# Accumulating transfers for two of four weight sums and wide products in an FFN's first chunk, with a rearranged start and tail

## The chip, the cores and the metric

One core of a Trainium2 chip runs the kernel. Its engines are named as in the profile: PE (TensorE matmuls; PEld their weight loads), DVE (VectorE), ACT (ScalarE), POOL (GpSimd) and SP (SyncE, which issues most DMAs). The metric is the device time of one execution in microseconds; the median of 3 runs before the change is 2033.53 us.

## The reference

One layer of a hybrid encoder, batch 1, 512 tokens, width 2048, all in float32:

```
xn    = rms_norm(x, g1);  proj = xn @ w_in            (2048 -> 5120)
y_a   = silu(layer_norm(depthwise_conv31(u * sigmoid(gate))))   1024 channels
y_b   = neighbourhood_attention(q, k, v, rpb)                   16 heads of 64
x     = x + concat(rms_norm(y_a), rms_norm(y_b)) @ w_out
h     = rms_norm(x, g2) @ w_up                        (2048 -> 2 x 5632)
h     = depthwise_conv3(h);  h = silu(h_gate) * h_value
x     = x + h @ w_down                                (5632 -> 2048)
out   = rms_norm(x, g3)
```

## The kernel before

**Exact products.** A float32 operand is split into a high part `hi` that PE's fast format (fp32r) holds and a low part `lo`, the rest. A product is then three matmuls, hi·hi, hi·lo and lo·hi (`mm3`, L127, L128, L129). Weights arrive as tiles of 128x1024 (512 KB) by DMAs that SP issues; `parts` (L113 to L118) makes `hi` by an ACT copy (L116) and `lo` by a DVE subtraction (L117). Four buffers hold the split pairs, seven hold raw tiles and the sums `ws` that are made of them. A written-out list `plan` holds the weights of all products in the order of their use; `weights()` issues a load and its split three products ahead (AHEAD = 3). Small steps of other stages (statistics, norms) are generators; `tick` lets one step through behind a named matmul, and each `yield` in a generator leaves its rest to a later tick. `pin` fixes an instruction's place on its engine; the others are placed by a scheduler.

**Start (L214 to L255).** x arrives as 16 tiles of 128x512 (k = 0 to 15), each split by ACT (L249) and DVE (L250) with the gain g1, which a DMA of ACT's queue brings. The weights of the first two projections arrive in ten pieces, two of each size, between the tiles of x, and are split at L226 and L227. Idle matmuls (L236, L240) run on PE until the first pieces are there.

**group_a (L373 to L402)** makes the convolution branch's layer norm and RMS norm. Their sums over channels are made by PE (`rsqrt_steps`, L190), the root by DVE and ACT (L173 to L177), and a broadcast by PE (L207). Two yields stand ahead of the layer norm's root, and two (RA_AFTER) ahead of the RMS norm's.

**FFN.** 44 blocks f of 128 hidden channels, gate and value each, come in 11 chunks of four. The up-projection of an f is done by a scheme with seven products in place of eight: K is halved, the tokens are halved, and products c = 0 to 6 use the weights A22, s = A21 + A22 (L666), A21 + A11 (L668), A11, s + A11 (L673), A12 and s + A12 (L677). The sums are DVE additions of 128x1024. Two forms exist:

- `up_apart` (L793 to L832, used for f0 to f3): a product is 24 matmuls of 256 columns. Its bank is emptied by ACT copies (L823, L826) or DVE additions (L825 to L831). For f0 the first three products run side by side, since their inputs are still being made.
- `up` (L708 to L791, f4 on): the high and low parts of the input stand side by side in 512 columns, so that a product is 8 wide matmuls of 512 columns (L718) and 8 of 256 for the low weights (L724). Its result has two halves, which ACT copies (L750) and more DVE additions (L765 to L789) put together.

`hidden` (L844) multiplies with the norm's factor, applies the convolution over tokens (L838 to L840), the gate's Silu (L849) and the product (L850); `in_two` splits it into `hh` and `hl` (L855, L856). From f4 on, products of the down-projection of the chunk before stand between the up products (`behind`, `down`, L859 to L871): ACT copies a bank out and POOL issues a 256 KB DMA that adds it to the residual in DRAM (L871). The first of them follows the third product of f4.

**stats2 (L644 to L653)** makes the RMS norm ahead of the FFN; its steps run beside f0's products, and f0's results wait for its broadcast (L207, L211).

**Tail (L941 to L998).** The last down products of the first 384 tokens are added, and their norm's statistics made (`rsqrt_steps`, rstd3). Meanwhile the last 128 tokens are computed the other way round, as four banks `pt` of 128 tokens x 512 channels (L973 to L979). A step of `spread` behind each block of three matmuls makes the statistics and finishes the transposed output (`finish`: L935 on DVE, L932 and L933 on ACT and POOL; DMAs L937 and L939). The 128 tokens' squares are summed on ACT (L981), the root is made (L986 to L989, L173 to L177) and four tiles are scaled and written (L993 to L998).

Of the kernel before, what the change touches and what calls it, by code (L numbers as in the profile page):

```python
# [16 lines left out]
P = 128  # L17
# [37 lines left out]
RA_AFTER = 2  # L55

PCOLS = [("g1", KD), ("dww", NC_ * CK), ("dwb", NC_), ("lng", NC_), ("lnb", NC_), ("cog", NC_),
# [10 lines left out]
def layer(ctx: ExitStack, tc: tile.TileContext, xT, xG, w_in, w_v, w_out, w_up, w_down, par, tab, g3, out, last_out):  # L68
# [27 lines left out]
    pin(nc.scalar.dma_start(g1, par[:, POFF["g1"]:POFF["g1"] + KD]))  # L96
# [5 lines left out]

    ones_r = consts.tile([P, P], F32R, name="ones")
# [112 lines left out]
    early = [[], []]  # L216

    def piece(u, j, c0, c1):

        if c0 == 0:  # L220
            early[j].append((t4([P, U * P], "raw"), wpool.tile([P, U * P], F32R, tag="whi", name="whi", bufs=NW),
                             wpool.tile([P, U * P], F32R, tag="wlo", name="wlo", bufs=NW)))
        n = (NC_, 0)[j]
        raw, hi, lo = (t[:, c0 * P:c1 * P] for t in early[j][u])
        pin(nc.sync.dma_start(raw, w_in[n, :, (u * U + c0) * P:(u * U + c1) * P]))
        pin(nc.scalar.activation(hi, raw, AF.Copy))  # L226
        pin(nc.vector.tensor_sub(lo, raw, hi.bitcast(F32)))  # L227
# [4 lines left out]
    warm = t2("warm", F32R)  # L232
    pin(nc.vector.tensor_copy(warm.rearrange("p (i k) -> p i k", k=P), ones.unsqueeze(1).broadcast_to([P, S // P, P])))
    ps = psa.tile([P, 2, S], F32, tag="sc", name="idle")
    for n in (S, S) + 3 * (H,) + 3 * (H - 32,):
        pin(nc.tensor.matmul(ps[:, 0, :n], warm[:, :P], warm[:, :n], start=True, stop=True))  # L236
    for n in (S, S) + 4 * (H,):
        for j in range(2):
            rows = slice(j * DH, (j + 1) * DH)
            pin(nc.tensor.matmul(ps[:, j, :n], warm[rows, :P], warm[rows, :n], start=True, stop=True))  # L240


    pieces = {k: [(u, j, c0, c1) for j in range(2)]
              for k, u, c0, c1 in ((0, 0, 0, 2), (2, 0, 2, 4), (4, 0, 4, 8), (6, 1, 0, 4), (9, 1, 4, 8))}
    for k in range(KD):
        x1.append(t2("x"))
        last = pin(nc.sync.dma_start(x1[k], xG[k]))
        h, l = t2("xh", F32R), t2("xl", F32R)
        pin(nc.scalar.activation(h, x1[k], AF.Copy, scale=g1[:, k:k + 1]))  # L249
        pin(nc.vector.scalar_tensor_tensor(l, x1[k], g1[:, k:k + 1], h.bitcast(F32), op0=ALU.mult, op1=ALU.subtract))  # L250
        xs.append((h, l))
        for c in pieces.get(k, ()):
            piece(*c)
# [73 lines left out]
    def project_first():  # L327
# [4 lines left out]
        for kk in range(KD):  # L332
            for j in range(2):
                m = mm3(both[j], early[j][kk // U][1:], kk % U, xs[kk][0], xs[kk][1], kk == 0, kk == KD - 1)
            if kk % 4 == 3:
                tick(m)
# [35 lines left out]
    def group_a():  # L372
# [15 lines left out]
        yield  # L388
        yield
# [9 lines left out]
        for _ in range(RA_AFTER):  # L399
            yield  # L400
# [243 lines left out]
    def stats2():  # L644
# [8 lines left out]
        rstd2.append((yield from rsqrt_steps(acc2, D, "rstd2", free=True, rest=2)))  # L653

    def factors(f):
# [4 lines left out]

        def make(c):
            if c == 0:
                return load(A22)
            if c == 1:
# [128 lines left out]
    def up_apart(f, between):  # L793

        def begin(c):
            return weights(), (psa.tile([P, S], F32, tag="po", name="pu") if c == 6 else
# [47 lines left out]
    def hidden(f, between):  # L844
        g, v = (up_apart if f < CH else up)(f, between)
# [33 lines left out]

    for c in range(NCH):  # L880
        hs = []
        for i in range(CH):

            last = c == NCH - 1 and i == CH - 1
            if c and i == CH - 1:
                hs = [in_two(h) for h in hs]
            hs.append(hidden(c * CH + i, lambda at: None if last else behind(c, i, at)))
# [185 lines left out]
```

## Time and profile before

| what | value |
|---|---|
| median of 3 runs | 2033.53 us (2030.55 to 2034.37) |
| profiled execution | 2030.16 us |
| its span | 2028.4 us |
| granted TensorE clock, mean | 0.998 |
| ACT busy | 1050.9 us (52%) |
| POOL busy | 159.5 us (8%) |
| HBM | 220.04 MB read, 54.53 MB written |

The span is the time from the first to the last record of the profiled execution; the rest of its time lies around it. A row of the timeline has the start and the duration in us, the engine, the line and the operation, output <- input with sizes, the count of instructions that follow one another, and in brackets the idle time before it and what ended that. A row of a group has the count, the busy time in us, the mean in ns, and the idle time before it. A row of the waits has total us, times, and the longest. A matmul's duration includes its way through the array, so the pace of PE is read from the starts: 0.227 us for 512 columns and 0.12 us for 256.

### The profile page before, as it was taken

Reading aid. Unit: us, or ns where it says so; the run is one execution under the profiler, and the core shown is the slowest. Engines: PE = TensorE matmul, PEld = TensorE weight load, DVE = VectorE, ACT = ScalarE, POOL = GpSimd, SP = SyncE. Lnnn points to the kernel's source line nnn. Section 1 sums busy time; section 2 is a strip of 40 time slices with the busy share of each in tenths; the row PEclk is TensorE's granted clock in tenths of the full one; section 3 lists DMA queues with packets and bytes.
Section 4 is the critical chain, followed back from the end, with each engine's and each line's share of the span. In section 5 each row is a group of like instructions: output and inputs, shape, how many; then the busy total and the mean of one; then the engine's idle time right before and its main releaser. Section 6 shows DMA issues by size and latency. Waiting matters only on the chain.

```text
span 2028.4 us, 28313 instructions
## 1 busy us (share of the span) xinstructions
PE 2015.4 (99%) x10672; PEld 1726.5 (85%) x10672; DVE 1675.5 (83%) x2298; ACT 1050.9 (52%) x1674; POOL 159.5 (8%) x188
## 2 busy tenths in 40 slices
PE   9999999999999999999999999999999999999998
PEld 7888888888888998888888888888888888888887
DVE  7986888988577898888888888888888888889875
ACT  7323344466346555555555555555555555555563
POOL 0000000000001001111111111111111111110111
PEclk9999999999999999999999999999999999999999
DMA  7232333336347435566565565565565565564583
GB/s 256 83 104 84 114 94 109 109 124 215 108 120 178 120 114 146 123 147 146 125 146 146 128 142 146 128 142 146 121 149 146 125 146 146 127 144 127 144 206 126
DMA packets 97784, 276.41 MB, mean 136 GB/s; under 512 B 10992, under 2 KB 12784, under 8 KB 97648
## 3 DMA queue, kind: packets, MB, share of 16 engines
q1 hardware_dynamic: 72288, 228.45, 36.3%
q0 software_dynamic: 25216, 46.15, 15.5%
q8 instruction: 84, 1.38, 0.3%
q14 instruction: 52, 0.43, 0.1%
q10 hardware_dynamic: 144, 0.01, 0.0%
HBM read 220.04 MB, written 54.53 MB: 135 GB/s over the span
## 4 chain that ended last, share of the span: by engine, by line
PE 96%; DVE 2%; DMA 1%; ACT 0%; issue 0%; SPq 0%; ACTq 0%; DVEq 0%
PE pu L718 25%; PE pu L724 13%; PE pd L129 8%; PE pd L127 8%; PE pd L128 8%; PE pj L127 5%; PE pj L128 5%; PE pj L129 5%; PE po L127 3%; PE po L128 2%; PE po L129 2%; PE pv L313 1%; PE pv L312 1%; PE pv L314 1%; PE pu L127 1%; PE pu L129 1%
## 5 line engine op out<-in xcount | busy, mean ns | idle before, releaser
L116 ACT ACTIVATE whi<-raw 128x1024 fp32r<-128x1024 f32 x364 | 384.4, 1058 | 503.8 <-PE pj L128 136.6
L117 DVE TENSOR_TENSOR wlo<-raw,whi 128x1024 fp32r<-128x1024 f32 x364 | 444.4, 1221 | 214.0 <-ACT whi L116 205.2
L718 PE MATMUL pu<-xc,whi 128*128 128x512 f32 x2240 | 552.9, 391 | 0.0
L718 PEld LDWEIGHTS pu<-xc,whi 128*128 128x128 f32 x2240 | 413.0, 188 | 79.1
L724 PEld LDWEIGHTS pu<-xc,wlo 128*128 128x128 f32 x2240 | 292.3, 191 | 13.9
L724 PE MATMUL pu<-xc,wlo 128*128 128x256 f32 x2240 | 296.6, 283 | 0.0
L129 PE MATMUL pd<-hh,wlo 128*128 128x512 f32 x640 | 250.1, 391 | 0.0
L127 PE MATMUL pd<-hh,whi 128*128 128x512 f32 x640 | 249.6, 390 | 0.0
L128 PE MATMUL pd<-hl,whi 128*128 128x512 f32 x640 | 249.3, 390 | 0.0
L871 POOL DMA_DIRECT2D x2d<-pdc x160 | 139.4, 873 | 1162.4 <-ACT pdc L870 837.4
L128 PE MATMUL pj<-xl,whi 128*128 128x512 f32 x512 | 200.2, 391 | 0.1
L129 PE MATMUL pj<-xh,wlo 128*128 128x512 f32 x512 | 200.0, 391 | 0.0
L127 PE MATMUL pj<-xh,whi 128*128 128x512 f32 x512 | 198.9, 393 | 0.0
L750 ACT ACTIVATE pl<-pu 128x256 f32<-128x256 f32 x280 | 104.6, 382 | 143.5 <-PE pu L718 136.4
L116 ACT ACTIVATE whi<-ws 128x1024 fp32r<-128x1024 f32 x132 | 139.8, 1059 | 75.2 <-PE pu L718 58.2
L366 DVE SCALAR_TENSOR_TENSOR y<-ch,prm,y 128x500 f32<-128x500 f32 (+14 forms) x240 | 173.3, 740 | 4.3
L117 DVE TENSOR_TENSOR wlo<-ws,whi 128x1024 fp32r<-128x1024 f32 x132 | 161.1, 1220 | 13.9 <-ACT whi L116 13.6
L129 PEld LDWEIGHTS pd<-hh,wlo 128*128 128x128 f32 x640 | 120.1, 188 | 28.5 <-DVE wlo L117 3.3
L128 PEld LDWEIGHTS pd<-hl,whi 128*128 128x128 f32 x640 | 120.2, 188 | 24.9 <-DVE hl L856 0.3
L127 PEld LDWEIGHTS pd<-hh,whi 128*128 128x128 f32 x640 | 120.4, 188 | 22.6
L870 ACT ACTIVATE pdc<-pd 128x512 f32<-128x512 f32 x160 | 93.8, 588 | 79.3 <-PE pd L129 65.9
L127 PEld LDWEIGHTS pj<-xh,whi 128*128 128x128 f32 x512 | 96.3, 188 | 20.7 <-ACT xh L249 0.2
(204 smaller groups left out, 2886.4 us busy)
## 6 DMA issues: line engine op xcount, KB each, us to landing
raw<-in_w_up SPq DMA_DIRECT2D x176, 512.0 KB, 3.7
raw<-in_w_down SPq DMA_DIRECT2D x88, 512.0 KB, 4.0
x2d<-pdc POOLq DMA_DIRECT2D x160, 256.0 KB, 4.8
raw<-in_w_in SPq DMA_DIRECT2D x60, 512.0 KB, 3.8
raw<-in_w_out SPq DMA_DIRECT2D x32, 512.0 KB, 3.8
raw<-in_w_v SPq DMA_DIRECT2D x16, 512.0 KB, 4.1
tab<-in_tab SPq DMA_DIRECT2D x32, 256.0 KB, 5.0
x<-in_xG SPq DMA_DIRECT2D x16, 256.0 KB, 5.4
```

Source lines behind the costliest of these rows:

```text
L116: i = nc.scalar.activation(hi[:, :n], raw[:, :n], AF.Copy)
L117: j = nc.vector.tensor_sub(lo[:, :n], raw[:, :n], hi[:, :n].bitcast(F32))
L127: nc.tensor.matmul(ps, hi[:, a], mh, start=start, stop=False)
L128: nc.tensor.matmul(ps, hi[:, a], ml, start=False, stop=False)
L129: return nc.tensor.matmul(ps, lo[:, a], mh, start=False, stop=stop)
L312: nc.tensor.matmul(ps, xh, wh[:, f], start=kk == 0, stop=False)
L366: nc.vector.scalar_tensor_tensor(y[:, a:b], h[:, a + j - PAD:b + j - PAD], prm[:, o + j:o + j + 1], y[:, a:b], op0=ALU.mult, op1=ALU.add)
L718: i = nc.tensor.matmul(ps, w[0][:, k * P:(k + 1) * P], comb[c][k], start=k == 0, stop=stop and k == ks[-1])
L724: i = nc.tensor.matmul(ps[:, H:], w[1][:, k * P:(k + 1) * P], comb[c][k][:, :H], start=False, stop=stop and k == U - 1)
L750: nc.scalar.activation(to, ps, AF.Copy)
L870: nc.scalar.activation(t, ps, AF.Copy)
L871: nc.gpsimd.dma_start(xd[d], t, accum_op=ALU.add)
```

## The change

Six parts:

1. **Start.** g1 is joined to the first tile of x (128x528, one DMA); ACT's DMA goes. The first split's high part is made by DVE. The weights of the first two projections lie interleaved in a new array `w_a` and come in five DMAs for k = 0, 1 to 3, 4 to 7, 8 to 11 and 12 to 15, issued behind x0, x1, x2, x6 and x10. The idle matmuls are six of 512 and one of 256 columns.
2. **group_a.** Three yields ahead of the layer norm's root in place of two; one ahead of the RMS norm's in place of two.
3. **stats2 and f0.** stats2's broadcast is four ticks behind its root in place of two. f0's gating and convolution are issued behind the second product of f1. f0's product c = 3 uses a bank of the pool "po" (before, c = 6 did).
4. **Wide products** (`up`) for f1 to f3.
5. **Sums by transfers** for f0 to f3: A22 is loaded a second time, into `ws`, and POOL issues two accumulating DMAs of 512 KB, A21 onto `ws` and A11 onto A21's tile. The DVE additions L666 and L668 go for these f.
6. **Tail.** The four banks alternate between two pools; the statistics' last part and all of `finish` come from the third bank's third step on, two calls a step; the sum of the first three squares stands ahead of the third bank's gain; the last root is written out, with a factor of -0.5 beside the square root.

```diff
+    xg0 = t4([P, U * P], "raw")[:, :S + KD]
+    pin(nc.sync.dma_start(xg0, x0))
...
-    pieces = {k: [(u, j, c0, c1) for j in range(2)]
-              for k, u, c0, c1 in ((0, 0, 0, 2), (2, 0, 2, 4), (4, 0, 4, 8), (6, 1, 0, 4), (9, 1, 4, 8))}
+    pieces = {0: (0, 1), 1: (1, 4), 2: (4, 8), 6: (8, 12), 10: (12, 16)}
...
-        yield
-        yield
+        for _ in range(3):
+            yield
         r = yield from rsqrt_steps(acc, CONV, "rln")
...
-        for _ in range(RA_AFTER):
-            yield
+        yield
         ra.append((yield from rsqrt_steps(acc, CONV, "ra")))
...
-        rstd2.append((yield from rsqrt_steps(acc2, D, "rstd2", free=True, rest=2)))
+        rstd2.append((yield from rsqrt_steps(acc2, D, "rstd2", free=True, rest=4)))
...
+        def sums():
+            a["s"] = t4([P, U * P], "ws")
+            nc.sync.dma_start(a["s"], w_up[f, A22])
+            nc.gpsimd.dma_start(a["s"], w_up[f, A21], accum_op=ALU.add)
+            load(A21)
+            nc.gpsimd.dma_start(a[A21], w_up[f, A11], accum_op=ALU.add)
+
         def make(c):
             if c == 0:
-                return load(A22)
-            if c == 1:
+                load(A22)
+                if f < CH:
+                    sums()
+                return a[A22]
+            if c == 1 and f < CH:
+                load(A11)
+            elif c == 2 and f < CH:
+                return a[A21]
+            elif c == 1:
                 a["s"] = t4([P, U * P], "ws")
                 add(a["s"], load(A21), a[A22])
...
-            return weights(), (psa.tile([P, S], F32, tag="po", name="pu") if c == 6 else
+            return weights(), (psa.tile([P, S], F32, tag="po", name="pu") if c == (6 if f else 3) else
...
     def hidden(f, between):
-        g, v = (up_apart if f < CH else up)(f, between)
+        return gated_tile(f, *up(f, between))
+
+    def gated_tile(f, g, v):
...
+    def meanwhile(c, i, at):
+        if (c, i, at) == (0, 1, 1):
+            hs[0] = gated_tile(0, *hs[0])
+        behind(c, i, at)
...
+            if not c and not i:
+                hs.append(up_apart(0, lambda at: None))
+                continue
...
-        elif (g, k) == (1, 0):
+        elif (g, k) == (2, 2):
...
-        elif rb and pairs:
-            at = pairs.pop(0)
+        for at in pairs[:2 if rb else 0]:
+            pairs.remove(at)
             finish(at, rb[at % 3 == 1], at % 3 == 1, at % 3 != 1)
...
-    root(r, y, v)
+    nc.scalar.activation(r, v, AF.Sqrt)
+    nc.vector.tensor_scalar(v, v, -0.5, None, op0=ALU.mult)
+    nc.vector.reciprocal(r, r)
+    nc.vector.scalar_tensor_tensor(y, r, v, r, op0=ALU.mult, op1=ALU.mult)
+    nc.vector.scalar_tensor_tensor(y, y, 1.5, r, op0=ALU.add, op1=ALU.mult)
```

More of the change, by code (lines that the diff above doesn't have):

```diff
@@ L215, in layer @@
     acc1 = t2("acc1")
[L216 to L227, printed above, removed]
+    early = []
@@ new lines, in layer, with piece @@
+    xg0 = t4([P, U * P], "raw")[:, :S + KD]
+    pin(nc.sync.dma_start(xg0, x0))
+    def piece(k0, k1):
+        if k0 % CH == 0:
+            early.append((t4([P, U * P], "raw"), wpool.tile([P, U * P], F32R, tag="whi", name="whi", bufs=NW),
+                          wpool.tile([P, U * P], F32R, tag="wlo", name="wlo", bufs=NW)))
+        o = k0 // CH * U * P
+        pin(nc.sync.dma_start(early[-1][0][:, 2 * k0 * P - o:2 * k1 * P - o], w_a[:, 2 * k0 * P:2 * k1 * P]))
+        for k in range(k0, k1):
+            if k % 2 and k > k0:
+                continue
+            raw, hi, lo = (t[:, 2 * k * P - o:2 * min(k // 2 * 2 + 2, k1) * P - o] for t in early[-1])
+            pin(nc.scalar.activation(hi, raw, AF.Copy))
+            pin(nc.vector.tensor_sub(lo, raw, hi.bitcast(F32)))
@@ L251, in layer @@
         xs.append((h, l))
-        for c in pieces.get(k, ()):
-            piece(*c)
+        if k in pieces:
+            piece(*pieces[k])
+        if k == 0:
+            pin(nc.vector.tensor_copy(g1, xg0[:, S:]))
     with tc.issue_after(last.ins):
```

60 lines of the change are left out of this document (33 added, 27 removed).

## The prediction

> **What bounds the kernel now.** First the profiled page: its busy line, the chain that ended last, and the loads of weights.
>
> ```profile
> PE 2015.4 (99%) x10672; PEld 1726.5 (85%) x10672; DVE 1675.5 (83%) x2298; ACT 1050.9 (52%) x1674; POOL 159.5 (8%) x188
> ...
> PE 96%; DVE 2%; DMA 1%; ACT 0%; issue 0%; SPq 0%; ACTq 0%; DVEq 0%
> ...
> raw<-in_w_up SPq DMA_DIRECT2D x176, 512.0 KB, 3.7
> ```
>
> TensorE (PE) is busy 99% of 2028.4 us and is 96% of the chain. So a change pays only where PE stands still, or where its own matmuls become fewer or shorter. An average of 83% on VectorE (DVE) hides stages, so I next cut the FFN's first chunk into windows: the third to seventh product of f0, f1 to f3, and the wide f4 up to its first down products.
>
> ```profile
> core 0: us, PE busy (x) PEld busy (x) DVE busy (x) ACT busy (x) POOL busy (x), PEclk, DMA share, GB/s
> ...
> 680.60:692.80 12.20, 12.19 (x102) 12.19 (x103) 9.95 (x17) 4.88 (x7) 0.00 (x0) 1.00 0.30 86
> 692.80:754.30 61.50, 61.45 (x510) 61.19 (x510) 60.87 (x79) 32.47 (x41) 0.00 (x0) 1.00 0.36 112
> 754.30:766.30 12.00, 12.00 (x66) 10.19 (x65) 11.83 (x17) 9.62 (x16) 0.00 (x0) 1.00 0.29 89
> ```
>
> Here both engines are full: DVE works 60.87 of 61.50 us beside f1 to f3. Over the 85.7 us it is busy 9.95 + 60.87 + 11.83 = 82.65 and idle 3.05. The waits of 676 to 768 us and the chain in it show where PE and DVE meet:
>
> ```profile
> PE pu L127 <- ACT vv L823: 1.5, 1, 1.5
> PEld pd L128 <- DVE hl L856: 0.3, 1, 0.3
> ...
> 680.61 0.39 PE pu L127
> 681.11 0.12 PE pu L129
> ...
> 754.48 2.07 PE pu L718 x9
> 756.55 1.91 PE pu L724 x16
> ```
>
> PE loses one block of 1.5 us ahead of 680.61: f0's fourth product waits for a bank that ACT empties. And at the first down products it already waits 0.3 us for a `hl` of DVE: the two engines arrive there together.
>
> **The change, part by part.** All terms are against the profiled execution, 2030.16 us (span 2028.4 and 1.8 around it); the median of the three runs is 2033.53, to which I apply the sum at the end.
>
> (a) *PE's own work in chunk 0.* f0's fourth product goes to another, free bank: -1.5 to -1.7. The wide form replaces 24 matmuls of 256 columns by 8 of 512 and 8 of 256: 8 x 2.07/9 + 8 x 1.91/16 = 2.80 us a product, against 24 x 0.12 = 2.88. The window 692.80 to 754.30 holds 21 apart products with two broadcasts of 0.23, (61.5 - 0.5)/21 = 2.90. So 21 x 0.10 = -2.1 at most, -1.7 at least. Alone PE would gain 3.2 to 4.2 us.
>
> (b) *DVE's work there.* The groups of 692.8 to 754.3, and two starts on DVE:
>
> ```profile
> L666 DVE TENSOR_TENSOR ws<-raw 128x1024 f32<-128x1024 f32 x3 | 3.7, 1218 | 0.0
> L668 DVE TENSOR_TENSOR raw<-raw 128x1024 f32<-128x1024 f32 x3 | 3.7, 1217 | 0.0
> L825 DVE TENSOR_TENSOR vl<-vv,pu 128x512 f32<-128x512 f32 x3 | 2.0, 681 | 0.0
> L827 DVE TENSOR_TENSOR uu<-uu,pu 128x256 f32<-128x256 f32 x3 | 1.2, 414 | 0.0
> ...
> 685.19 1.23 DVE L117 TENSOR_TENSOR wlo<-ws,whi 128x1024 fp32r<-128x1024 f32 x1 [1.13 <-ACT whi L116]
> ...
> 691.47 1.23 DVE L117 TENSOR_TENSOR wlo<-raw,whi 128x1024 fp32r<-128x1024 f32 x1 [1.13 <-ACT whi L116]
> ```
>
> Taken away: L666 and L668 for f1 to f3, 6 x 1.22 = 7.3 us by duration (f0's own pair lies before 680). Added: the wide form's results come in two parts, and the code has 4 additions of 512 and 7 of 256 columns for each f where the apart form has 2 and 4. So 3 x (2 x 0.68 + 3 x 0.41) = 7.8 us. DVE's work is therefore not smaller; **the adds that the transfers take over pay for the wide form's additions and no more**. What DVE can gain is idle time: two gaps of 1.13, behind splits of weights that came late because PE stood still until 680.61. With (a) those splits are issued up to 1.7 us earlier. I let DVE keep 1.5 us of idle and work 0.1 more by pitch: it finishes the last `hl` of the chunk about 1.5 us earlier:
>
> ```profile
> 761.33 0.68 DVE L856 TENSOR_TENSOR hl<-uy,hh 128x512 fp32r<-128x512 f32 x1
> ...
> 765.54 0.68 DVE L856 TENSOR_TENSOR hl<-uy,hh 128x512 fp32r<-128x512 f32 x1
> ```
>
> The last moves from 765.54 to about 764.0. PE, 3 to 4 us ahead by (a), waits for it and for the `wlo` of the down weights that stand among these four. So chunk 0 is worth what DVE gains: **-1.5**, bounds 0 (DVE keeps all its idle) and -4.2 (DVE does not hold PE). f0's gating is moved behind f1's second product on the same engine; it changes the order, not the amount.
>
> (c) *The eight accumulating transfers.* 512 KB each from GpSimd, with one more 512 KB load an f. The nearest rows are the 160 of 256 KB; the line of L871 on issue, and its landing:
>
> ```profile
> L871 POOL DMA_DIRECT2D x2d<-pdc x160: 862/865/1172, 771.2 to 1974.0; - x160
> ...
> DMA to landing us min/median/max: 3.8/4.8/8.4
> ...
> 686.61 1.06 ACT L116 ACTIVATE whi<-ws 128x1024 fp32r<-128x1024 f32 x1 [0.50 <-PE pu L128]
> ...
> 705.84 1.05 ACT L116 ACTIVATE whi<-ws 128x1024 fp32r<-128x1024 f32 x1
> ```
>
> A `ws` buffer is free when its split ends, at 687.7, and the sum for it is read first at 705.84: 18.2 us for a load (3.7) and an accumulation. At the median's 4.8 to twice that, 9.6, it is there 5 us early: cost 0. At twice the worst, 16.8, it would be 2.3 late. GpSimd has nothing else there but the last squares of stats2, behind which one accumulation stands. DMA share is 0.36 in that window, so the added bytes have room. I take 0.
>
> [...]
>
> (d) *Start.* The first product pair now waits for fewer, other pieces.
>
> ```profile
> 5.52 0.42 ACT L226 ACTIVATE whi<-raw 128x256 fp32r<-128x256 f32 x1 [0.73 <-DMA raw<-in_w_in]
> ...
> 6.05 0.80 PE L127 MATMUL pj<-xh,whi 128*128 128x512 f32 x1
> ...
> 7.07 0.63 PE L129 MATMUL pj<-xh,wlo 128*128 128x512 f32 x1
> 7.50 0.51 PE L127 MATMUL pj<-xh,whi 128*128 128x512 f32 x1
> ...
> 8.31 0.63 PE L127 MATMUL pj<-xh,whi 128*128 128x512 f32 x2
> ...
> 11.06 0.62 PE L127 MATMUL pj<-xh,whi 128*128 128x512 f32 x2
> ...
> 16.50 0.71 PE L127 MATMUL pj<-xh,whi 128*128 128x512 f32 x2
> 17.26 0.50 PE L128 MATMUL pj<-xl,whi 128*128 128x512 f32 x1
> ...
> 9.19 1.38 ACT L249 ACTIVATE xh<-x,g 128x512 fp32r<-128x512 f32 x2
> ...
> 8.31:30.00 21.69, 21.63 (x95) 17.40 (x94) 19.89 (x31) 19.48 (x32) 0.00 (x0) 1.00 1.04 387
> ```
>
> Without the wait for g1 and with a smaller first piece, k=0 no longer waits for a second piece (5.52) and begins 1 to 1.5 us earlier; k=1 about 0.5 (it needs the 384 KB piece). But x3 now stands behind 2056 KB in place of 1536; at 387 GB/s that is 1.3 us later than 9.19, and ACT splits two weight pieces ahead of it. k=3 begins near 11.9 in place of 11.06 (+0.85); the stall behind 16.50 (two matmuls of 0.23, then nothing until 17.26: 0.3, and 0.1 in the next) has then no reason, so some 0.45 of it stays. I take **+0.3**, bounds -0.6 (k=1's gain is kept) and +1.3.
>
> (e) *group_a's statistics* move one tick later. The wait it had:
>
> ```profile
> 432.07 1.05 PE L190 MATMUL st<-ones,acc 128*128 128x1 f32 x8 [0.31 <-DVE acc L170]
> ```
>
> Its PE pitch had a hole of 0.47 there; **-0.4**, bounds -0.5 and 0 (0: the wait is only moved; the norm behind it gives up one of its own two ticks).
>
> (f) *Tail.* The finishing products of out_T begin later, two a step.
>
> ```profile
> 2014.47 2.71 DVE L935 SCALAR_TENSOR_TENSOR fin<-x,prm,st 128x384 f32<-128x384 f32 x5 [0.56 <-ACT rb L966]
> ...
> 2017.23 0.69 DVE L984 TENSOR_TENSOR xg<-pt,g3b 128x512 f32<-128x512 f32 x1
> ...
> 2020.45 0.16 DVE L989 SCALAR_TENSOR_TENSOR rsv<-rsl,rsv 128x1 f32<-128x1 f32 x1
> 2020.65 0.20 ACT L173 ACTIVATE rsr<-rsv 128x1 f32<-128x1 f32 x1 [0.59 <-DVE rsv L989]
> ```
>
> Before, two of ten were done ahead of 2014.47. Now all ten follow: from about 2014.2, 10 x 0.54 + 0.69 + 2 x 0.15 = 6.4, so the last sum starts at 2020.7 and not 2020.45. The root behind it has one dependent DVE step less (0.1 to 0.2). **+0.1**, bounds -0.4 and +0.5.
>
> Sum: -1.5 + 0 + 0.3 - 0.4 + 0.1 = -1.5 us, 2028.7 for a profiled execution like this one, **2032.0** against the median of 2033.53.
>
> **The rivals.** *1, PE's whole gain:* DVE is not in PE's way, because the splits' order leaves it time. For it: only 0.3 us of waiting for `hl` is on record. Against: DVE's 60.87 of 61.50. Then -4.2 - 0.4 + 0.1, and 0 to -0.6 at the start: about -4.8, 2028.7.
> *2, slower: the accumulations come late.* The mechanism is (c): DVE's and ACT's splits of the sum stand in order ahead of all later splits, so lateness goes straight to PE. It decides from 14.5 us (18.2 - 3.7) an accumulation. At 16.8 each of the three f's loses 2.3: +6.9 on -1.5 = +5.4, 2038.9. For it: nothing of 512 KB on this queue is in the trace. Against: 8.4 is the worst of 160. [...]
> *3, the start slips:* x3 comes at the upper bound and PE, whose matmuls come at 0.43 (7.07 to 7.50) at the start and at 0.23 later, stays slow longer: 1.0 more on the forecast and no gain in chunk 0 (+1.5): +1.0, 2034.5.
> *4, the change does not do what it says:* f1's bank is freed by a DVE addition ordered behind two splits, so that the stall of f0 only moves to f1: chunk 0 gains 0, sum 0, 2033.5.
>
> **How the numbers follow.** About 0.2%, 4.1 us, is what a measurement of this kernel tells from no change. Forecast 0.50, rival 1 0.22, rival 2 0.10, rival 3 0.10, rival 4 0.08. Faster by over 0.2% (under 2029.5): most of rival 1 and a little of the forecast, 0.25. Slower (over 2037.6): rival 2 and a part of 3, 0.13. Within: 0.62. The range goes from rival 1 with all other lower bounds, -4.2 - 0.6 - 0.5 - 0.4 = -5.7, 2027.8, to the sum of the upper bounds, 0 + 1.3 + 0 + 0.5 = 1.8, with 1 us of a late accumulation in one f: 2036.3. That leaves out rival 2's and the far ends, some 2 in 10.
>
> **What would show it.** In the changed profile: no wait of PE on `vv` in f0's fourth product; f4 beginning 3 to 4 us earlier against f0 than before, and then PE waiting 1 to 3 us for `hl` or `wlo` at the first down products; DVE idle under 2 us in f1 to f3; accumulations landing in under 12 us with no split waiting for them. Wrong would be: no PE wait at the first down (rival 1), ACT or DVE idle behind a transfer in f1 to f3 (rival 2), k=3 after 12.5 us (rival 3), a new wait on a bank in f1 (rival 4).

## The result, and the profile after

The kernel after takes **2036.61 us** (median of 16 runs, 2035.1 to 2039.68) against 2030.55 us of the kernel before on the same chip (16 runs, 2029.81 to 2034.37): ratio 1.0029, interval 1.0022 to 1.0036. It is slower by 6.1 us, where 1.5 us less was forecast. The forecast was counted from a median of 3 runs that lies 3 us above the one of 16 runs; so the time itself is only 0.3 us above the range, but the change is 3.3 us above the range's upper end of +2.8.

The profiled execution after took 2036.23 us. Its busy line:

```profile
span 2034.5 us, 28023 instructions
...
PE 2015.0 (99%) x10491; PEld 1717.3 (84%) x10491; DVE 1672.8 (82%) x2306; ACT 1055.6 (52%) x1691; POOL 166.9 (8%) x196
```

PE is as busy as before (2015.0 against 2015.4) although it issues 181 matmuls less, and the span has grown by 6.1: nothing was added to PE's work, but it stands still longer and, as shown below, runs at a granted clock of 0.50 for a while. To find where, I took the start of the first and the last matmul of each stage from PE's timeline of both kernels and subtracted:

```
stage                              before     after   difference
first product                        6.05      4.38      -1.67
first score product                237.64    237.82      +0.18
last projection of L127 to L129    478.45    477.92      -0.53
last score product                 523.00    528.01      +5.00
first product of f0                670.29    675.29      +5.00
first down product                 762.68    766.38      +3.70
last up product                   1949.72   1955.34      +5.62
last matmul of the tail           2018.94   2024.58      +5.64
span                              2028.4    2034.5       +6.1
```

So the start costs 0.2, group_a's first root gives 0.7 back, **a place near 500 us costs 5.5**, chunk 0 of the FFN costs 0.6 (1.3 gained up to the first down product, 1.9 lost behind it), and the end, behind the last matmul, 0.45.

**Near 500 us.** PE's part of the timeline after; the brackets hold the idle time and what ended it:

```profile
499.20 0.39 PE L128 MATMUL po<-mal,whi 128*128 128x512 f32 x1
499.42 0.39 PE L129 MATMUL po<-mah,wlo 128*128 128x512 f32 x1
501.22 0.73 PE L207 MATMUL st<-dg,ones 128*128 128x512 f32 x2 [1.41 <-ACT ao L512]
503.37 0.79 PE L127 MATMUL po<-mah,whi 128*128 128x512 f32 x1 [1.41 <-DVE oa L590]
503.96 0.63 PE L128 MATMUL po<-mal,whi 128*128 128x512 f32 x1
504.38 0.63 PE L129 MATMUL po<-mah,wlo 128*128 128x512 f32 x1
```

Two waits: the broadcast of the RMS norm's factor (L207) waits for a bank that an ACT copy (`ao`, L512) empties, and the next product of the output projection for a bank that DVE (L590) empties. DVE's row there reads the factor's copy `ra`, so this wait is for ACT too:

```profile
502.62 1.29 DVE L590 TENSOR_TENSOR oa<-po,ra 128x512 f32<-128x512 f32 x2
```

By the starts the first takes 501.22 - 499.42 - 0.227 = 1.57; the second, behind the second matmul of L207 at 501.56, takes 503.37 - 501.56 - 0.227 = 1.58. Behind them the matmuls come at 0.42 (503.96 to 504.38), twice the pace of the two ahead (0.22). The granted clock, from the windows:

```profile
core 0: us, PE busy (x) PEld busy (x) DVE busy (x) ACT busy (x) POOL busy (x), PEclk, DMA share, GB/s
499.40:503.40 4.00, 1.18 (x5) 0.34 (x3) 2.63 (x4) 2.77 (x4) 0.00 (x0) 0.91 0.94 347
503.40:509.50 6.10, 6.10 (x14) 4.75 (x15) 3.00 (x5) 0.00 (x0) 0.00 (x0) 0.50 0.21 81
```

PEclk is 0.50 in these 6.1 us: some 13 matmuls lose 0.2 each, 2.6 us. With the waits that is 5.7, the 5.5 of the table. What ACT did meanwhile, first after, then before:

```profile
499.62 1.06 ACT L116 ACTIVATE whi<-raw 128x1024 fp32r<-128x1024 f32 x1 [1.72 <-PE po L128]
500.59 0.58 ACT L512 ACTIVATE ao<-po 128x512 f32<-128x512 f32 x1
501.20 0.63 ACT L169 ACTIVATE sq<-ao 128x512 f32<-128x512 f32 x1
501.99 0.60 ACT L211 ACTIVATE ra<-st 128x512 f32<-128x512 f32 x1 [0.16 <-PE st L207]
```

```profile
497.83 0.58 ACT L507 ACTIVATE ao<-po 128x512 f32<-128x512 f32 x1
498.44 0.63 ACT L169 ACTIVATE sq<-ao 128x512 f32<-128x512 f32 x1
499.84 0.60 ACT L211 ACTIVATE ra<-st 128x512 f32<-128x512 f32 x1 [0.76 <-PE st L207]
500.77 1.06 ACT L116 ACTIVATE whi<-raw 128x1024 fp32r<-128x1024 f32 x1 [0.33 <-PE po L128]
```

The four instructions are the same, but their order is not. Before, the split of the next weights (`whi`) was the last of them; now it is the first. It needs a `whi` buffer that PE frees only with the L128 at 499.20, and ACT stood idle 1.72 for it with `ao` queued behind. `ao`, and then the factor's copy `ra`, came 2.8 and 2.2 us later, and PE, which had freed the buffer for the split, waited for both copies.

**Chunk 0.** The waits of PE on `vv` in f0's fourth product are gone. Others stand in the waits of 676 to 770 us (total us, times, longest):

```profile
PE st L207 <- DVE dg L201: 1.6, 1, 1.6
PE pd L129 <- DVE wlo L117: 1.6, 1, 1.6
```

The first is stats2's broadcast. DVE's timeline ahead of it, and PE's:

```profile
698.89 0.69 DVE L197 TENSOR_TENSOR dg<-ident,rsy 128x512 fp32r<-128x512 f32 x1
699.51 1.23 DVE L117 TENSOR_TENSOR wlo<-ws,whi 128x1024 fp32r<-128x1024 f32 x1
700.65 1.13 DVE L201 SCALAR_TENSOR_TENSOR dg<-ident,rsy,dg 128x128 fp32r<-128x128 f32 x4
```

```profile
699.72 0.47 PE L207 MATMUL st<-dg,ones 128*128 128x512 f32 x1 [0.44 <-DVE dg L197]
701.84 0.51 PE L207 MATMUL st<-dg,ones 128*128 128x512 f32 x1 [1.65 <-DVE dg L201]
```

PE reached the broadcast before DVE had made its two parts, between which a 1.23 us split of weights stands: 0.6 and 1.9 us by the starts. For the whole chunk I set the same stretch of both kernels side by side, from 10.3 us behind f0's first product to the end of the chunk's last `hl`: first before, then after.

```profile
680.60:766.20 85.60, 85.54 (x673) 83.51 (x674) 82.55 (x111) 46.97 (x64) 0.00 (x0) 1.00 0.34 105
```

```profile
685.60:771.40 85.80, 82.11 (x492) 72.46 (x491) 83.76 (x121) 50.34 (x80) 3.55 (x4) 1.00 0.49 138
```

PE's busy time fell by 3.4 us. DVE's rose by 1.2 and its idle time fell only from 3.05 to 2.04, so that the stretch, which ends with an instruction of DVE, became 0.2 us longer.

**The accumulating transfers** land in time; the two lines of the DMA view, from the source views of L669 and L671, are

```profile
DMA to landing us min/median/max: 6.8/7.1/7.5
```

```profile
DMA to landing us min/median/max: 6.7/7.9/10.7
```

and no split of a sum waits for a DMA. The first four transfers, issued up to 668 us beside a DVE that is 57 to 88% busy, land in 6.7 to 7.2 us; the last four, issued from 695 us on beside a DVE that is 96 to 97% busy, in 7.0 to 10.7. The two slowest also follow another accumulation by 2 to 3 us, so the runs don't tell which of the two makes them late.

### The profile page after: what moved, and what is told of

Read it like the earlier page. It is cut to its first block, busy times and chain, and to the rows that moved or that the text cites. A ratio compares the mean times of both kernels' runs of the same rounds, so it can differ in the third digit from the quotient of the medians.

```text
span 2034.5 us, 28023 instructions
## 1 busy us (share of the span) xinstructions
PE 2015.0 (99%) x10491; PEld 1717.3 (84%) x10491; DVE 1672.8 (82%) x2306; ACT 1055.6 (52%) x1691; POOL 166.9 (8%) x196
## 4 chain that ended last, share of the span: by engine, by line
PE 98%; DVE 1%; ACT 0%; DMA 0%; issue 0%; SPq 0%; ACTq 0%; DVEq 0%
PE pu L737 26%; PE pu L743 14%; PE pd L129 8%; PE pd L127 8%; PE pd L128 8%; PE pj L127 6%; PE pj L128 6%; PE pj L129 6%; PE po L127 3%; PE po L128 3%; PE po L129 3%; PE pv L319 1%; PE pv L318 1%; PE pv L320 1%; PE po L506 1%; PE trp L491 1%
## 5 line engine op out<-in xcount | busy, mean ns | idle before, releaser
L737 PE MATMUL pu<-xc,whi 128*128 128x512 f32 x2408 | 593.5, 391 | 0.0
L737 PEld LDWEIGHTS pu<-xc,whi 128*128 128x128 f32 x2408 | 443.8, 188 | 85.3 <-issue 0.2
L743 PEld LDWEIGHTS pu<-xc,wlo 128*128 128x128 f32 x2408 | 314.1, 191 | 14.9
L743 PE MATMUL pu<-xc,wlo 128*128 128x256 f32 x2408 | 318.8, 282 | 0.0
L128 PE MATMUL pd<-hl,whi 128*128 128x512 f32 x640 | 249.1, 390 | 0.0
L128 PE MATMUL pj<-xl,whi 128*128 128x512 f32 x512 | 200.3, 391 | 0.1
L769 ACT ACTIVATE pl<-pu 128x256 f32<-128x256 f32 x301 | 112.7, 382 | 159.1 <-PE pu L737 150.5
L128 PEld LDWEIGHTS pd<-hl,whi 128*128 128x128 f32 x640 | 120.2, 188 | 24.8 <-DVE hl L877 0.2
```

What stands on the lines that cost most here:

```text
L128: nc.tensor.matmul(ps, hi[:, a], ml, start=False, stop=False)
L737: i = nc.tensor.matmul(ps, w[0][:, k * P:(k + 1) * P], comb[c][k], start=k == 0, stop=stop and k == ks[-1])
L743: i = nc.tensor.matmul(ps[:, H:], w[1][:, k * P:(k + 1) * P], comb[c][k][:, :H], start=False, stop=stop and k == U - 1)
L769: nc.scalar.activation(to, ps, AF.Copy)
```

## The experiments

Each was timed in five rounds beside the kernel before on the same chip. Spans and stage differences are those of its profiled execution against the profile of before. The experiments were made in four batches, in which the median of the kernel before is 2030.08 to 2030.37 us; a difference between two batches is uncertain by about as much. Diffs are against the kernel that is named.

**Theory A and its rivals: the place near 500 us.** A says that the order of ACT, which the yields decide, makes the 5.5 us. Rivals: a bank shared by `ao` and the broadcast (B), or something else of the change. (The letters of the expectations differ: e1 and e2 call any other edit B, and e3 and e4 still take the bank to be a part of A.)

*e1: after, with group_a's yields as before.*

```diff
-        for _ in range(3):
-            yield
+        yield
+        yield
         r = yield from rsqrt_steps(acc, CONV, "rln")
...
-        yield
+        for _ in range(2):
+            yield
         ra.append((yield from rsqrt_steps(acc, CONV, "ra")))
```

> The changed kernel with group_a's ticks as before: two ahead of the layer norm's root, two ahead of the RMS norm's. Theory A (the one tick that group_a moved puts a split of weights ahead of the copy that frees the bank of the broadcast, PE waits 1.6 and 1.6 us there and then runs 6 us at half clock): the two waits and the half clock near 500 us go, and the time falls by 5 to 5.5 us, to about 2031. Rival B (the loss near 500 us comes from the start or from another edit that shifts everything): less than 1 us changes.

Measured: 2032.87 us, ratio 1.0010 (1.0001 to 1.0018), 3.7 less than after. Near 500 us PE has no wait but one of 0.3, which before has too, and its clock is 1.00 (495 to 515 us); ACT's order is that of before. The stage difference there is -0.2 from the start to f0. So the yields are the cause of that loss; but the total is still 2.7 over before, since chunk 0 now costs +2.7. There the broadcast's two waits are 1.3 and 1.9 us, and the clock falls too:

```profile
694.00:698.00 4.00, 1.26 (x4) 0.67 (x4) 3.97 (x11) 0.99 (x4) 0.32 (x1) 1.00 1.01 254
698.00:701.10 3.10, 3.10 (x13) 2.79 (x12) 2.82 (x4) 1.86 (x3) 0.00 (x0) 0.50 1.05 272
```

*e2: before, with the yields of after alone* (the reverse of e1's edit, in before).

> The kernel before with nothing but group_a's ticks changed, three and one in place of two and two. Theory A: it alone makes the waits and the half clock near 500 us, less the 0.5 us that it saves at 432 us: slower than before by 4.5 to 5 us. Rival B: within 1 us of the kernel before, or 0.4 us faster as the prediction had it.

Measured: 2033.35 us, ratio 1.0014 (1.0005 to 1.0023), span 2032.3. The two waits are there, 1.57 and 1.58, and a granted clock of 0.58 from 503.40 to 507.50 us: stage difference +3.8 at the last score product. The yields alone are enough.

*e3: after, with the broadcast of `ra` in another pool's bank.*

```diff
-        ra.append((yield from rsqrt_steps(acc, CONV, "ra")))
+        ra.append((yield from rsqrt_steps(acc, CONV, "ra", free=True)))
```

> The changed kernel, its ticks kept at three and one, but the RMS norm's broadcast of group_a writes a bank of the score pool in place of the bank that the attention's copy still holds. Theory A (the bank is what PE waits for): no wait of PE near 500 us, clock kept, time lower by 5 to 5.5 us, as with the ticks put back. Rival C (DVE's statistics are late with one tick less): the wait stays at the broadcast and only its releaser changes; under 1 us gained.

Measured: 2037.43 us (2034.91 in the profiled execution), ratio 1.0031 (1.0022 to 1.0041), span 2033.1. L207 waits no more, but the next product does, as long as both waits together:

```profile
503.37 0.50 PE L127 MATMUL po<-mah,whi 128*128 128x512 f32 x1 [3.39 <-DVE oa L590]
```

Theory B falls: the bank only decided where PE stood. What holds it is the factor's copy behind the split on ACT, as in after.

*e4: after, three yields ahead of the first root and two ahead of the second.*

```diff
-        yield
+        for _ in range(2):
+            yield
         ra.append((yield from rsqrt_steps(acc, CONV, "ra")))
```

> The changed kernel with three ticks ahead of the layer norm's root and two ahead of the RMS norm's, so that the broadcast comes a product later, when the attention's copy is done. Theory A: no wait near 500 us, 5 to 5.5 us faster than the changed kernel. Rival D (three products' results then wait for the factor, so that PE waits for their banks instead): a wait of about a product's remainder, 2 to 5 us, stands there in its place.

Measured: 2039.85 us, ratio 1.0043 (1.0029 to 1.0056). Three waits now (the diagonals of L197 and L201, then L590), 5.5 us together, and a granted clock of 0.75 (499.40 to 513.00 us): +5.8 between the first and the last score product. One tick more is not a small thing in either direction. Two yields and one, the remaining combination, wasn't run.

*e13: after, with `ao` held ahead of the split on ACT* (an order of these two instructions alone; `ao5` is the copy `ao`, the 83rd split is the one near 500 us, and `issue_after` holds an instruction behind another).

```diff
...
-        i = nc.scalar.activation(hi[:, :n], raw[:, :n], AF.Copy)
+        count[0] += 1
+        if count[0] in (83,) and ao5:
+            with tc.issue_after(ao5[0].ins):
+                i = nc.scalar.activation(hi[:, :n], raw[:, :n], AF.Copy)
+        else:
+            i = nc.scalar.activation(hi[:, :n], raw[:, :n], AF.Copy)
...
```

> The changed kernel, ticks kept at three and one, with one constraint more: on ACT the split of weights that stood ahead of the attention's copy near 500 us is issued behind it. Theory A' (ACT's order): the broadcast no longer waits for the copy; the factor's own copy still stands behind the split, so one wait of about 2 us stays where there were two of 1.6 with a stretch at half clock. 1 to 3.5 us faster than the changed kernel. Rival (something else holds PE there): within 0.5 us of it.

Measured: 2036.62 us, ratio 1.0028 (1.0017 to 1.0038): no gain in the median. ACT's and PE's rows:

```profile
497.99 0.58 ACT L519 ACTIVATE ao<-po 128x512 f32<-128x512 f32 x1
499.79 1.06 ACT L121 ACTIVATE whi<-raw 128x1024 fp32r<-128x1024 f32 x1 [1.22 <-PE po L135]
...
501.27 0.58 ACT L218 ACTIVATE ra<-st 128x512 f32<-128x512 f32 x1
```

```profile
499.81 0.63 PE L214 MATMUL st<-dg,ones 128*128 128x512 f32 x2
503.36 0.50 PE L134 MATMUL po<-mah,whi 128*128 128x512 f32 x1 [2.92 <-DVE oa L599]
```

`ao` and the broadcast are early, but `ra` still stands behind the split, and PE waits for it in one piece. Together with e3: it is `ra` behind a split that waits for PE. Taking `ra` alone ahead of the split wasn't tried by itself; e1 does it together with `ao`.

**Chunk 0.** Theory E: PE's new wait is the broadcast, so a later broadcast gains it. Theory F: DVE sets the end of the chunk.

*e5: e1, with the broadcast kept until the fourth product of f1 and f0's gating behind it.*

```diff
-        rstd2.append((yield from rsqrt_steps(acc2, D, "rstd2", free=True, rest=4)))
+        rstd2.append((yield from rsqrt_steps(acc2, D, "rstd2", free=True, rest=6)))
...
-        if (c, i, at) == (0, 1, 1):
+        if (c, i, at) == (0, 1, 3):
             hs[0] = gated_tile(0, *hs[0])
```

(The matmuls of f1's products and of the broadcast are also held in this order.)

> Base is e1 (group_a's ticks put back). The broadcast of the FFN's norm is held on PE until the fourth product of f1 is done, two products later, and f0's gating follows it. Theory E (the wait of 1.3 and 1.9 us for DVE's diagonal at this broadcast is a loss of its own): the wait and the half clock behind it go and the time falls by 3 to 4.5 us against e1, to 2028.5 to 2030. Rival F (the prediction's: DVE sets the end of the chunk): the wait at the first down products grows by what the broadcast no longer costs, and less than 1 us is gained.

Measured: 2037.18 us, ratio 1.0033 (1.0020 to 1.0046), 4.3 worse than e1. The broadcast waits no more, but f1's products wait for banks that hold unscaled results (3.0 us for `g` L854, 2.0 for `uu` L796), and the stretch of chunk 0 grows from 88.0 to 91.8 with the same DVE work (83.64). A later broadcast is no remedy; whether the wait itself is a loss is settled by e9 and e10. (1.0 us of this trace stands ahead of the first score product, where its clock is at 0.50 from 8.6 to 12.0 us.)

*e6: e1, with the sums of weights of f0 to f3 on DVE again* (`f < CH` becomes `f < 0` in `make`; the wide products stay).

> Base is e1; DVE makes all four sums of f0 to f3 again, the eight accumulating transfers are gone, the wide products of f1 to f3 stay. Theory F (DVE sets the end of the chunk): the six additions of 1.14 us come back whole, 5 to 7 us slower than e1. Theory E (PE's waits are set by the order at the broadcast): 0 to 2 us slower.

Measured: 2037.80 us, ratio 1.0031 (1.0019 to 1.0043), 4.9 worse than e1. DVE's busy time in the stretch is 87.89 against 83.80: the transfers take 4.1 us off DVE here. The stretch is 3.0 us longer in the trace (91.0 against 88.0) and the time 4.9 in the median, a little under theory F's 5 to 7 and far from its rival's 0 to 2: with the wide form the end follows DVE.

*e7: e1, with f1 to f3 apart again, the transfers kept.*

```diff
-        return gated_tile(f, *up(f, between))
+        return gated_tile(f, *(up_apart if f < CH else up)(f, between))
```

> Base is e1; f1 to f3 use the apart form again, the accumulating transfers stay, so that DVE has 6.6 us less to do than in e1 and PE 2.1 us more. Theory F: the wait at the first down products goes (-1.8), that at the broadcast shrinks, PE's own work grows by 2.1: 0 to 2 us faster than e1. Rival G (DVE is not what PE waits for): 2 us slower than e1.

Measured: 2034.38 us, ratio 1.0017 (1.0008 to 1.0025); in the trace 0.7 better than e1, in the median 1.5 worse, so no clear difference. DVE works 4 us less than in e1 (79.74) and PE still waits 0.7 and 0.9 us at the broadcast and 1.6 for a `wlo` at the first down products. Here the load of DVE is not the reason, since it is idle for 7 of 86.7 us; its order is, split after split ahead of the steps of the root. e10 below changes that order alone.

*e9: e1, with stats2's root and diagonals placed ahead of splits on DVE* (a scheduler priority) and so made before PE needs them.

```diff
-        nc.vector.tensor_scalar(v, ps, 1.0 / n, EPS, op0=ALU.mult, op1=ALU.add)
-        root(r, y, v)
...
+        with shifted(-400 if name == "rstd2" else 0):
+            nc.vector.tensor_scalar(v, ps, 1.0 / n, EPS, op0=ALU.mult, op1=ALU.add)
+            root(r, y, v)
...
```

> Base is e1; DVE's root and diagonal of the FFN's norm are placed ahead of the splits of weights, and the order that results has the broadcast on PE one product later. Theory H (the wait at the broadcast is a loss by the order on DVE, not by DVE's amount of work): the wait of 3.1 us and the half clock behind it go, and 2.5 to 4.5 us are gained against e1. Rival F (DVE sets the end): the wait at the first down products grows instead, under 1 us gained.

Measured: 2033.50 us, ratio 1.0015 (1.0006 to 1.0024), the same as e1. The wait at the broadcast is gone and the first down product comes 3.3 us earlier than before; there PE waits for DVE and gives back more than all of it:

```profile
759.41 0.63 PE L127 MATMUL pd<-hh,whi 128*128 128x512 f32 x2
761.34 0.73 PE L128 MATMUL pd<-hl,whi 128*128 128x512 f32 x2 [1.30 <-DVE hl L879]
763.68 0.80 PE L129 MATMUL pd<-hh,wlo 128*128 128x512 f32 x1 [1.61 <-DVE wlo L117]
764.28 0.63 PE L127 MATMUL pd<-hh,whi 128*128 128x512 f32 x1
```

```profile
700.00:754.30 54.30, 53.49 (x309) 47.12 (x308) 54.26 (x77) 31.21 (x51) 1.76 (x2) 1.00 0.50 146
754.30:770.00 15.70, 12.79 (x54) 10.26 (x53) 15.70 (x21) 10.09 (x17) 0.00 (x0) 0.78 0.21 68
```

DVE is busy 69.96 of these 70 us. Theory F holds: with wide products in f1 to f3, PE's gain is real and DVE doesn't let it through. The clock falls here as well (0.78; starts 0.43 apart from 764.28 on): by the last up product PE is 2.9 us behind before, and of the 6.1 us lost since the first down product the two waits are 3.2 by the starts and the clock the rest.

*e10: e9, with f1 to f3 apart* (e7's edit).

> As e9, and f1 to f3 in the apart form (as in e7), with the accumulating transfers. Theory H: against e7 the 1.5 us at the broadcast go; faster than e7 by 1 to 2 us, and near the kernel before, within 1 us of it. Rival F: DVE has 6.6 us less to do than in e9, so this is 2 us or more faster than e9.

Measured: 2028.98 us, ratio 0.9993 (0.9984 to 1.0002). No wait of PE over 0.25 us is left in chunk 0, and the last up product comes 2.2 us earlier against f0's first than before. Against e7, from which it differs in the order on DVE alone, it is 5.4 us faster in the median and 3.9 in the span: the broadcast's wait was a loss, and with it gone f0's other bank pays what it was worth. Against before the gain is 1.6 us in the span; the interval still holds no change.

*e11: e1, with f0's banks as before* (`c == 6` in place of `c == (6 if f else 3)`).

> Base is e1; f0's fourth product takes the bank it took before, so that PE waits 1.7 us there again. Theory I (the wait at the broadcast is what the removed wait turned into): the broadcast's wait of 3.1 us and the half clock go and the time is 1 to 3 us lower than e1 although a wait was put in. Rival: both waits stand, 1.7 us slower.

Measured: 2032.20 us (2030.96 in the profiled execution), ratio 1.0008 (0.9999 to 1.0017). PE's old wait of 1.5 for `vv` is back and the broadcast's is gone; chunk 0 costs 0.4 in place of 2.7 in that trace. In the median the kernel takes 0.7 less than e1, which the intervals don't tell from nothing. A wait put back costs nothing, since PE would stand at the broadcast instead.

*e12: before, with the transfers alone* (`sums` and `make` of the change).

> The kernel before with nothing but the sums of f0 to f3 by accumulating transfers. Theory F (DVE sets the end of the chunk): DVE loses 6 x 1.14 us of work there and PE's waits of 0.5 us in the chunk go: 0.3 to 0.7 us faster, no more since PE waits no longer. Rival (late accumulations or the extra 2 MB of loads cost time): slower by over 1 us. The trace says whether any split waits for such a transfer.

Measured: 2030.25 us, ratio 0.9996 (0.9987 to 1.0005). DVE's busy time in the stretch falls from 82.55 to 78.27; PE, which sets the end here, gains 0.1 in chunk 0: its wait of 0.3 for `hl` is gone.

**Start and tail.**

*e8: e1, with the tail of before.*

> Base is e1; the tail of the kernel before. By the traces of before, after and e1, the tail costs 0.45 us from PE's last matmul to the end of the span; with the old one the time falls by 0.3 to 0.6 us. Rival: the new tail is as good as the old and the difference is the pace of the last writes: within 0.2 us.

Measured: 2033.23 us, ratio 1.0012 (1.0004 to 1.0021), span 2031.4 as e1. The expected 0.3 to 0.6 did not come. From the last matmul to the issue of the last write the new tail takes 5.2 us and the old one 5.4, in every trace; the medians don't show these 0.2. The 0.45 us that after loses at its end come later, while the four last writes land. Their line in the DMA view of before, and then the one that after and e8 both have:

```profile
DMA to landing us min/median/max: 3.0/3.2/3.4
```

```profile
DMA to landing us min/median/max: 3.5/3.6/3.9
```

*e16: before, with the new start alone.*

> The kernel before with nothing but the new start. By the traces of e1 to e12 the new start puts the first score product between 0.2 us earlier and 1.3 us later than before, depending on when PE's clock rises: 0 to 0.6 us slower in the median. The prediction had +0.3, bounds -0.6 and +1.3.

Measured: 2031.34 us against 2030.08, ratio 1.0005 (0.9996 to 1.0014). The first score product comes only 0.1 later, but the span is 1.1 us longer, and 0.9 of that lies behind the last matmul, in a tail that this kernel does not change. Its last writes land in 3.5 to 3.8 us. So do those of all 13 kernels with the new start (3.5 to 3.9), with either tail, and those of the five with the old start in 3.0 to 3.4: **the slower end comes with the new start**. By what way a start reaches the last writes is open; among other things it brings two new arrays in DRAM.

**The version that the experiments point to**: before, with f0's bank, its late gating, the broadcast four ticks behind the root, and e9's order of DVE; f1 to f3 apart; start, group_a and tail as before.

*e14: this, with the transfers.*

> The kernel before with the sums of f0 to f3 by transfers, f0's fourth product in the other bank, f0's gating behind f1's second product, and the norm's root placed ahead of the splits on DVE; apart form for f1 to f3, start, group_a and tail as before. Theory H and F together: the 1.7 us wait of f0 goes and nothing takes its place: 1.9 to 2.4 us faster than the kernel before. Rival: the wait comes back at the broadcast or at the down products, within 0.7 us of the kernel before.

Measured: 2028.37 us, ratio 0.9991 (0.9982 to 0.9999): 1.7 us faster in the median, where 1.9 to 2.4 were expected. No wait of PE over 0.25 us is left in chunk 0.

*e15: this, without them.*

> As e14 but with all sums on DVE. Theory F (DVE has no room in the chunk): without the transfers DVE's 83.8 us of work set the end again and the wait of f0 turns into a wait at the down products: 0 to 0.7 us faster than the kernel before, 1.3 to 2 us slower than e14. Rival: the same as e14 within 0.3 us, and the transfers are worth nothing.

Measured: **2027.86 us**, 2027.33 to 2028.09, ratio 0.9984 (0.9976 to 0.9993): faster than before by 2.2 us and than after by 8.7. All 11 runs lie below the lowest of the kernel before in its batch (29 runs, 2029.38). Chunk 0 in windows:

```profile
680.60:692.80 12.20, 12.20 (x104) 12.20 (x103) 11.66 (x21) 6.39 (x10) 0.00 (x0) 1.00 0.33 98
692.80:754.30 61.50, 61.50 (x505) 61.04 (x504) 61.13 (x79) 32.35 (x42) 0.00 (x0) 1.00 0.37 113
754.30:764.00 9.70, 9.70 (x55) 8.48 (x55) 9.70 (x14) 6.82 (x10) 0.00 (x0) 1.00 0.20 61
```

PE is busy in every microsecond, and DVE in all but 0.9 of 83.4. I had thought that the root's early place would need the DVE time that the transfers free; it doesn't. f0's late gating and the broadcast's two more ticks came along and were not tested by themselves, nor was the new tail without the new start.

## Why the prediction was wrong

In the profiled executions it had -1.5 and the span grew by 6.1. The step that failed by most is (e): it priced a moved tick by the wait that it removes (-0.4) and put its effect on the order of the other engines at nothing; the runs have +4.8. The second is in (b), rows counted as removed that are not. The terms, in the prediction's order:

- **(a) and (b), chunk 0: -1.5 forecast, +0.6 measured** (+2.7 in e1). (a) held: the wait of 1.7 us is gone, and PE's own work fell by 2.1, within the 1.7 to 2.1 forecast (from f0's first product to the first down product 92.4 us with that wait before, 91.1 with the broadcast's 2.5 after). These two terms add up to 3.2 to 3.8; the 4.2 with which the prediction goes on, in (b)'s bound and in rival 1, is not their sum. That DVE, not PE, decides held too (e9). The step that failed here is in (b): "Taken away: L666 and L668 for f1 to f3, 6 x 1.22 = 7.3 us". The six rows of 692.8 to 754.3 are those of f2, f3 and f4, not of f1 to f3. Both timelines show it, before and then after:

```profile
658.68 1.23 DVE L666 TENSOR_TENSOR ws<-raw 128x1024 f32<-128x1024 f32 x1 [1.59 <-issue]
673.36 1.22 DVE L668 TENSOR_TENSOR raw<-raw 128x1024 f32<-128x1024 f32 x1 [0.78 <-DMA raw<-in_w_up]
...
745.52 1.22 DVE L666 TENSOR_TENSOR ws<-raw 128x1024 f32<-128x1024 f32 x1
749.48 1.22 DVE L668 TENSOR_TENSOR raw<-raw 128x1024 f32<-128x1024 f32 x1
```

```profile
753.87 1.22 DVE L685 TENSOR_TENSOR ws<-raw 128x1024 f32<-128x1024 f32 x1
757.87 1.22 DVE L687 TENSOR_TENSOR raw<-raw 128x1024 f32<-128x1024 f32 x1
```

  The last pair before and the only one left after is f4's, which no transfer replaces; f1's pair ran at 658 and 673, where DVE had idle time. So the transfers take 4 x 1.22 = 4.9 us from the stretch in which DVE is full (4.3 in e12, 4.1 between e6 and e1), against 7.8 added by the wide form: +2.9 and not +0.5. With the 1.5 us of idle time that I let go, the same sum would have been +1.4 and not -1.5. Measured, DVE's busy time rose by 1.2: one split of weights less falls into the stretch (1.2 us; 11 rows of `wlo<-ws` against 12), and the remaining 0.5 is overlap of rows, which a sum of durations counts twice. The idle time fell by 1.0 only. The two gaps of 1.13 are gone, but others of up to 0.66 have come; the broadcast is not their cause, since e11, where PE doesn't wait there, has 2.4 us of idle as well.

  The forecast's sign of f4 beginning 3 to 4 us earlier against f0 came out as 1.3: PE, freed from its bank, stands at stats2's broadcast, and e11, which puts the old wait back, has none there. Rival 4 named this kind of thing, a stall that only moves, but at f1's bank; it was the broadcast, made late on DVE, as e9 and e10 show. I had not asked what else in f0 waits for DVE once PE comes 1.7 us earlier.
- **(c) the transfers: 0 forecast, 0 measured.** Landings of 6.7 to 10.7 us lie under the 14.5 from which rival 2 begins, and no split waited for one. That a busy DVE makes them late was not shown: the last four landed in 7.0 to 10.7 us beside a DVE that was 96 to 97% busy, and the two slowest of them also follow another accumulation. So no run shows a reason for the one in ten of rival 2. e12 and e15 add that the transfers are worth nothing while PE sets the end.
- **(d) the start: +0.3 forecast, +0.2 measured at the first score product** (+0.1 in e16), **and some 0.5 more at the end of the kernel.** k=1 began at 7.90 against 8.31 (0.4 of the 0.5 that I gave it); k=3 came at 11.16 and not at 11.9, but its six matmuls took until 13.04, 0.6 behind before, of which 0.4 was made up by the next stall that did not come. Up to here the sum was right, its parts only nearly. Kernels with the same start come 0.3 us earlier to 1.3 later than before at the first score product; the two latest, e4 and e5, have a stretch of 3.4 us at a granted clock of 0.50 there (in e5 from 8.6 to 12.0 us). That the start also slows the last writes (e16) was in no term: with it the start costs about 0.7 in after and 1.1 in e16.
- **(e) group_a: -0.4 forecast, +4.8 measured; the largest failure.** The hole at 432 us went (-0.7, more than its bound of -0.5). But the term priced the wait that was removed, "0: the wait is only moved", and bounded what the tick does to its norm, not to the engine that it shares. The moved steps changed the scheduler's order of four instructions on ACT 70 us later, and put one that waits for PE ahead of two that PE waits for (e1, e2, e3, e13). Which of the two moved yields does it is open: with three and two (e4) the score products lose no less.
- **(f) the tail: +0.1 forecast (its own sum gives 2020.6, not 2020.7), -0.2 measured** from the last matmul to the issue of the last write. The time from the last matmul to the end grew by 0.45 all the same, but e8 with the old tail shows no less (0.65) and e16 more (0.9): that growth belongs to (d).

The range failed with (e): its bounds, -0.5 and 0, were those of the wait that was seen and left out an order that was not looked at. Rivals 1 and 2 are refuted (PE waits at the first down products; no transfer is late). Rival 3 did not come in after; of its slow start e4 and e5 show 1.3 and 1.0 us. Rival 4's wait on a bank in f1 did not come.

## What to carry to other kernels

A yield or tick moved by one is an edit of every engine's order: compare the instruction order of each engine from there on, and look for an instruction that waits for PE and now stands ahead of one that PE waits for. Before a group of rows is booked as removed, assign each row to its iteration, since work that is issued ahead belongs to a later one than the stage it runs beside. And where a stall of the main engine is removed, list what it reaches next and move that producer too: in e1 f0's bank was worth nothing (e11), with the root's steps ahead of the splits it gave e15 its 2 us. And an edit of the start can cost at the end: e16 lost 0.1 us where its edit is and 0.9 behind the last matmul.

## What the runs showed of the hardware

**PE's clock.** Two waits of PE of 1.6 us each, 0.6 us of work apart, brought its granted clock to 0.50 for 6.8 us in after (502.69 to 509.51). The same two waits in e2 brought it there for half as long, 3.4 us (503.51 to 506.93), so that a window of 4.1 us has 0.58. One wait of 3.4 in e3, at the same place, brought none. The windows of e2 and e3 are

```profile
503.40:507.50 4.10, 4.07 (x11) 3.22 (x12) 3.07 (x5) 0.00 (x0) 0.00 (x0) 0.58 0.30 120
```

```profile
503.40:509.50 6.10, 6.10 (x30) 5.08 (x31) 3.00 (x5) 0.58 (x1) 0.00 (x0) 1.00 0.20 75
```

In e13 a wait of 2.9 did again (starts at 0.43 from 504.52 on, and 0.72 in the window of 503.40 to 509.50), and in e1 waits of 1.3 and 1.9 (0.50 from 698.00 to 701.10), both for 3.4 us. So about 3 us of standing still cost 3.4 us in e3 and 5.7 in after. What decides between no lower clock, 3.4 us of it and 6.8 us the runs don't show.

In the traces of kernels with the same code in chunk 0 (after, e4, e3, e8, e13, e1) the chunk costs +0.6, four times +2.2, and +2.7. Three of those that cost more have a lower granted clock there: e8 with 0.96 from 670 to 700 us, e13 with 0.98 from 700 to 770, and e1 with the 0.50 above; after has 1.00 from 680.60 to 770.00. e1's runs reach from 2031.40 to 2035.87.
